# Encoder block, first stage: row scales from squares of the transposed x, and a new layout for x and the keys' weights

## Chip, core and metric

The kernel runs on one core of a Trainium2 chip. The metric is the device time of one execution in microseconds (us). The engines are TensorE (PE, whose weight loads the profile lists as PEld), VectorE (DVE), ScalarE (ACT), GpSimd (POOL) and SyncE (SP). Only SP issues transfers here, all on one queue that 16 DMA engines serve.

## What is computed

One encoder block over 512 tokens of width 1024 with 16 learned "meta" tokens ahead of them, in f32. The first stage is an RMS norm and a wide projection whose column blocks feed two attention branches; gates, a merge and a feed-forward part follow.

```python
def rms_norm(x, g):
    xf = x.astype(jnp.float32)
    y = xf * lax.rsqrt(jnp.mean(xf * xf, axis=-1, keepdims=True) + RMS_EPS)
    return (y * g.astype(jnp.float32)).astype(x.dtype)
...
    u = rms_norm(h, pre_mix_gain[l])
    proj = u @ w_in[l]
    qa, ka, va, qb, kb, vb, g = jnp.split(proj, SPLITS, axis=-1)
...
    o_swa = windowed_gqa_sink_attention(qa, ka, va, attn_sink[l], pos, is_real)
...
    o_diff = differential_attention(qb, kb, vb, lam, lambda_init, subln_gain, is_key)
    gates = jax.nn.sigmoid(g + b_gate[l])
    merged = g_swa * (o_swa @ w_branch_swa[l]) + g_diff * (o_diff @ w_branch_diff[l])
    h = h + rms_norm(merged @ w_out[l], post_mix_gain[l])
    u = rms_norm(h, pre_ffn_gain[l])
    gate_up = u @ w_ffn_in[l]
    f = (jax.nn.silu(gate_up[..., :D_FF]) * gate_up[..., D_FF:]) @ w_ffn_out[l]
    h = h + rms_norm(f, post_ffn_gain[l])
```

The row scale, one number per token, is the reciprocal root of the mean square of that token's 1024 values. It commutes with the projection, so the kernel multiplies the projected columns by it afterwards.

## The kernel before

**Products.** Every f32 operand is split into a high part of type F32R and a low part, the remainder; a product is three matmuls, high by high, high by low and low by high (`mm3`, lines 287 to 289). ACT makes the high part (`act.copy`, or `act.activation` with the gain), DVE or POOL the low part (`sub_hi`, line 253). The tokens stand transposed in `xh` and `xl` (128 partitions of features, 8 tiles of k, 528 columns: 16 meta tokens and 512 tokens).

**The front** is the part up to line 505, whose order is written out by hand for PE, ACT, DVE and SP. SP fetches the transposed x tile by tile (`x_load`, line 391, raw tiles `xr`, 264 KB each), and in between the weights of two column blocks of the keys (`w_part`, line 406). ACT and DVE split each x tile (`x_split`, lines 397 and 398) and each piece of the weights (line 257 on ACT, 253 on DVE). PE first runs 60 matmuls on a constant tile (line 380), then the keys' products k by k: 12 matmuls of 264 columns for each of 8 k (line 447), into three banks `pr` and one `Sw`. Then come the first value block with the weights `wV` (two halves `pV`, 48 matmuls) and the second with `wV2` (`pV2`, 48 matmuls).

**The row scales before.** SP fetches the 512 tokens a second time, not transposed (`xn`, line 419, four transfers of 512 KB), and the meta tokens (`xm`, line 420). ACT (line 460) and DVE (line 462) square them in turn and sum along each row into `ss`. `rsqrt_cols` (lines 306 to 318, DVE with one POOL power) turns the sums into scales; DVE spreads each over 128 columns (`rb`, lines 483 and 486) and PE transposes these into `rps` (lines 484 and 487), from where ACT copies them to `rbc`, the scale of each column.

**Behind the front** a planner takes over: `Plan` places tasks by modelled costs, by priorities and by the time at which each engine is taken to be free, a small table of numbers at the call. Its first tasks scale the value blocks by `rbc` (`VT`, line 589), transpose them on PE (lines 599 and 607), turn the keys by the rotary tables (`rope_t`, line 554 to 566), move them between partitions (`move`, line 576), fetch and split the query weights (`weights`, lines 527 and 529), and run the queries' products (512 columns a matmul). The first scores are the matmuls `Sw<-KK,Q` of line 715.

Of the kernel before, what the change touches and what calls it, by code (L numbers as in the profile page):

```python
# [237 lines left out]
def encoder(ctx, tc, I, out, dbg=None):  # L238
# [151 lines left out]
    def x_load(k):  # L390
        sp.dma_start(out=xr[k // 2][:, k % 2], in_=I["xT"][k])
        if k == 0:
            sp.dma_start(out=vec, in_=I["vec"])

    def x_split(k):
        r = xr[k // 2][:, k % 2]
        act.activation(out=xh[:, k, :], in_=r, func=AF.Copy, scale=mgain[:, k:k + 1])
        dve.scalar_tensor_tensor(out=xl[:, k, :], in0=r, scalar=mgain[:, k:k + 1],
                                 in1=xh[:, k, :].bitcast(F32), op0=ALU.mult, op1=ALU.subtract)

    def w_part(w, n, k0, k1):
        if k0 == 0:
            w.extend([wp.tile([P, KT, P], F32, tag="wr", name="wr", bufs=RB),
                      wp.tile([P, KT, P], F32R, tag="wh", name="wh"), wp.tile([P, KT, P], F32R, tag="wl", name="wl")])
        ks = slice(k0, k1)
        sp.dma_start(out=w[0][:, ks], in_=I["w_in"][n].rearrange("p (k c) -> p k c", k=KT)[:, ks])
        split(w[1][:, ks], w[2][:, ks], w[0][:, ks])

    wA, wB = [], []
    for k in range(KT):  # L410
        x_load(k)
        x_split(k)
        for k0, k1 in {0: ((0, 2),), 1: ((2, 4),), 3: ((4, KT),)}.get(k, ()):
            w_part(wA, 0, k0, k1)
            w_part(wB, 1, k0, k1)
    wA, wB = wA[1:], wB[1:]
# [22 lines left out]
    kB = [pr_t(HALF), Sw[0][:, 0:HALF]]  # L439
    halves = [slice(s * HALF, (s + 1) * HALF) for s in range(2)]  # L440
    for k in range(KT):
        todo = [(ps_, w[a][:, k, :], (xh, xl)[b][:, k, cs], k == 0 and a == b == 0, k == KT - 1 and a == 1)
                for hs, w in ((kA, wA), (kB, wB)) for ps_, cs in zip(hs, halves) for a, b in ((0, 0), (0, 1), (1, 0))]
        if k == 0:
            todo = [x for p in range(3) for x in todo[p::3]]
        for ps_, a, b, first, last in todo:
            pe.matmul(out=ps_, lhsT=a, rhs=b, start=first, stop=last)
# [8 lines left out]
    for t in range(5):
        src, n = (xn[:, t], P) if t < 4 else (xm, NMETA)
        jk = atp.tile([P, D], BF16, tag="rt", name="jk", bufs=RT)
        if t % 2 == 0:
            act.activation(out=jk[:n], in_=src, func=AF.Square, accum_out=ss[:n, t:t + 1])  # L460
        else:
            dve.tensor_tensor_reduce(out=jk[:n], in0=src, in1=src, scale=1.0, scalar=0.0,
                                     op0=ALU.mult, op1=ALU.add, accum_out=ss[:n, t:t + 1])
        if t == 0:
            for ps_, raw in ((kA, kraw[0]), (kB, kraw[1])):
                for s in range(2):
                    act.copy(out=raw[:, halves[s]], in_=ps_[s])
    pV2 = [pr_t(HALF), pr_t(HALF)]

    def v2(h, ks):  # L470
        for k in ks:
            mm3(pV2[h], (wV2[0][:, k, :], wV2[1][:, k, :]), (xh[:, k, halves[h]], xl[:, k, halves[h]]), k == 0, k == KT - 1)

    ks = [slice(h * KT // 2, (h + 1) * KT // 2) for h in range(2)]
    for h in range(2):
        act.copy(out=wV2[0][:, ks[h]], in_=rV2[:, ks[h]])
    rst = rsqrt_cols(const, ss, P, 1.0 / D, "r0",
                     between=lambda: sub_hi(wV2[1][:, ks[0]], rV2[:, ks[0]], wV2[0][:, ks[0]]))
    v2(0, range(KT // 2))
    rps = ps.tile([P, 512], F32, tag="av", name="rps")  # L480
    for t in range(4):
        rb = atp.tile([P, P], F32, tag="rt", name="rb", bufs=RT)
        dve.tensor_copy(out=rb, in_=rst[:, t:t + 1].broadcast_to([P, P]))
        pe.transpose(out=rps[:, t * P:(t + 1) * P], in_=rb, identity=ident)
    rb = atp.tile([P, P], F32, tag="rt", name="rb", bufs=RT)
    dve.tensor_copy(out=rb, in_=rst[:, 4:5].broadcast_to([P, P]))
    pe.transpose(out=Sw[1][:, 0:P], in_=rb, identity=ident)
    sub_hi(wV2[1][:, ks[1]], rV2[:, ks[1]], wV2[0][:, ks[1]])
    v2(0, range(KT // 2, KT))
    v2(1, range(KT))  # L490
# [1119 lines left out]
```

## Time and profile before

| what | value |
|---|---|
| time, median of 3 runs | 949.36 us (948.16 to 950.43) |
| time of the profiled execution | 949.22 us |
| its span, first to last instruction | 947.4 us |
| PE busy / DVE busy / ACT busy / POOL busy | 931.6 / 716.2 / 525.8 / 216.0 us |
| mean granted TensorE clock | 0.996 |
| fetched and moved by DMA | 110.46 MB, mean 117 GB/s |

Times in the rows of the trace count from the span's start. A row of the timeline gives start, duration, engine, line, operation, output and inputs, shapes, and in brackets the idle time ahead of it with what ended that idle time. Matmuls overlap, so the distance of two starts is what one costs. A duration of DVE or ACT is likewise longer than the distance to the next start.

### The profile page before, as it was taken

The numbers are of one execution on the slowest core, as the hardware profiler recorded it, in microseconds if no ns is written. First come the engines' busy times: TensorE is split into PE (matmuls) and PEld (weight loads), VectorE is DVE, ScalarE is ACT, GpSimd is POOL, SyncE is SP. The second block draws the span as 40 slices with busy tenths as digits, with TensorE's granted clock in tenths as the row PEclk, the third lists the DMA queues.
The fourth block names the chain that finished last, engine by engine and source line by source line (L and its number), as shares of the span: only waits on it lengthen the run. The fifth ranks groups of instructions, "written<-read, shape, count | busy, mean of one in ns | idle before, by whom it ended". The sixth has DMA issues, their size and how long they took to land.

```text
span 947.4 us, 15653 instructions
## 1 busy us (share of the span) xinstructions
PE 931.6 (98%) x5871; PEld 834.1 (88%) x5871; DVE 716.2 (76%) x1234; ACT 525.8 (55%) x957; POOL 216.0 (23%) x228
## 2 busy tenths in 40 slices
PE   9999999999999999999999999999999999999996
PEld 9788879889898999999888888998999999988885
DVE  5738898999564759877773865886787887799975
ACT  7337766775644446667556443654555555565541
POOL 0544455543222433243211421300000000000000
PEclk9999999999999999999999999999999999999999
DMA  9483132251425144433532460364323333180122
GB/s 319 160 220 102 51 104 58 63 148 45 123 89 157 46 122 127 105 96 115 157 112 67 161 216 23 100 186 141 117 104 101 117 95 112 46 333 13 55 67 89
DMA packets 38011, 110.46 MB, mean 117 GB/s; under 512 B 6177, under 2 KB 7457, under 8 KB 37937
## 3 DMA queue, kind: packets, MB, share of 16 engines
q1 hardware_dynamic: 37792, 109.34, 38.1%
q8 instruction: 46, 0.75, 0.3%
q14 instruction: 29, 0.23, 0.1%
q10 hardware_dynamic: 144, 0.13, 0.0%
HBM read 88.09 MB, written 2.10 MB: 95 GB/s over the span
## 4 chain that ended last, share of the span: by engine, by line
PE 86%; DVE 5%; DMA 4%; ACT 2%; issue 1%; SPq 1%; DVEq 0%; ACTq 0%
PE pr L287 19%; PE pr L289 19%; PE pr L288 19%; PE Sd L863 3%; PE wk L288 2%; PE wk L287 2%; PE wk L289 2%; PE Sw L715 2%; PE O L771 2%; PE tr L918 2%; PE Od L931 2%; PE tr L764 2%; DMA wr<-in_w_in_dram 2%; PE tr L288 1%; PE tr L287 1%; PE tr L289 1%
## 5 line engine op out<-in xcount | busy, mean ns | idle before, releaser
L287 PE MATMUL pr<-xh,wh 128*128 128x264 f32 (+1 forms) x592 | 193.4, 327 | 0.0
L289 PE MATMUL pr<-xh,wl 128*128 128x264 f32 (+1 forms) x592 | 190.0, 321 | 0.6 <-POOL wl L253 0.6
L288 PE MATMUL pr<-xl,wh 128*128 128x264 f32 (+1 forms) x592 | 189.8, 321 | 0.0
L253 POOL TENSOR_TENSOR wl<-wr,wh 128x1024 fp32r<-128x1024 f32 (+2 forms) x42 | 99.5, 2372 | 145.2 <-ACT wh L529 82.5
L289 PEld LDWEIGHTS pr<-xh,wl 128*128 128x128 f32 x592 | 111.6, 189 | 9.6 <-POOL wl L253 1.3
L288 PEld LDWEIGHTS pr<-xl,wh 128*128 128x128 f32 x592 | 111.9, 189 | 7.4
L287 PEld LDWEIGHTS pr<-xh,wh 128*128 128x128 f32 x592 | 111.8, 189 | 7.4 <-issue 0.2
L529 ACT CAST wh<-wr 128x1024 fp32r<-128x1024 f32 x56 | 58.5, 1048 | 47.0 <-PE pr L288 34.6
L309 POOL TENSOR_TENSOR r3y<-r3v,mhalf 128x1 f32<-128x1 f32 x4 | 2.2, 549 | 326.1 <-DVE r3v L308 326.1
L253 DVE TENSOR_TENSOR wl<-wr,wh 128x1024 fp32r<-128x1024 f32 (+2 forms) x61 | 69.0, 1134 | 10.0 <-ACT wh L272 8.2
L287 PE MATMUL pr<-TM,sx 128*128 128x256 f32 x236 | 66.9, 283 | 0.2 <-ACT s L1393 0.2
L289 PE MATMUL pr<-TM,sx 128*128 128x256 f32 x236 | 66.8, 283 | 0.0
L288 PE MATMUL pr<-TM,sx 128*128 128x256 f32 x236 | 66.8, 283 | 0.0
L868 DVE TENSOR_REDUCE nm<-Sd 128x1 f32<-128x528 f32 x64 | 45.1, 705 | 20.8 <-PE Sd L863 19.9
L253 DVE TENSOR_TENSOR sx<-S,sx 128x1024 fp32r<-128x1024 f32 x34 | 41.6, 1224 | 24.9 <-PE pr L288 12.7
L289 PE MATMUL pr<-uh,wl 128*128 128x256 f32 (+1 forms) x188 | 55.0, 292 | 0.4 <-DVE wl L253 0.4
L287 PE MATMUL pr<-uh,wh 128*128 128x256 f32 (+1 forms) x188 | 55.0, 293 | 0.0
L288 PE MATMUL pr<-ul,wh 128*128 128x256 f32 (+1 forms) x188 | 54.9, 292 | 0.0
L566 POOL TENSOR_TENSOR ta<-ta,tb 128x528 f32<-128x528 f32 (+1 forms) x26 | 37.0, 1422 | 74.5 <-DVE tb L554 45.3
L871 ACT ACTIVATE pp<-Sd,nm 128x528 f32<-128x528 f32 x40 | 27.9, 699 | 39.2 <-DVE pa L884 22.6
L257 ACT CAST sx<-S 128x1024 fp32r<-128x1024 f32 x34 | 35.7, 1050 | 25.1 <-PE pr L289 8.2
L729 POOL TENSOR_SCALAR p<-p,rc 128x272 f32<-128x272 f32 (+1 forms) x64 | 35.9, 573 | 47.9 <-DVE rc L727 44.5
(528 smaller groups left out, 2673.9 us busy)
## 6 DMA issues: line engine op xcount, KB each, us to landing
wr<-in_w_in_dram SPq DMA_DIRECT2D x50, 512.0 KB, 4.1
wg<-in_w_fi_dram SPq DMA_DIRECT2D x17, 512.0 KB, 3.6
wu<-in_w_fi_dram SPq DMA_DIRECT2D x17, 512.0 KB, 3.5
wr<-in_w_fi_dram SPq DMA_DIRECT2D x16, 512.0 KB, 3.8
b<-in_w_fo_dram SPq DMA_DIRECT2D x16, 512.0 KB, 8.5
Kd<-hl SPq DMA_DIRECT2D x32, 132.0 KB, 2.4
Kd<-Kd SPq DMA_DIRECT2D x16, 264.0 KB, 3.7
Q<-hl SPq DMA_DIRECT2D x64, 64.0 KB, 2.8
```

The costliest lines, as they stand in the source:

```text
L253: (eng or dve).tensor_tensor(out=lo, in0=src, in1=hi.bitcast(F32), op=ALU.subtract)
L257: act.copy(out=hi, in_=src)
L287: pe.matmul(out=ps, lhsT=ah, rhs=bh, start=first, stop=False, **more)
L288: pe.matmul(out=ps, lhsT=ah, rhs=bl, start=False, stop=False, **more)
L289: pe.matmul(out=ps, lhsT=al, rhs=bh, start=False, stop=last, **more)
L529: T("ACT", 1.05, lambda: act.copy(out=wh.t, in_=wr.t), r=[wr], w=[wh], prio=pr_)
L566: T("POOL", 0.05 + 1.3 * m, lambda: pool.tensor_tensor(out=ta.t[:, :, 0:n], in0=ta.t[:, :, 0:n], in1=tb.t[:, :, 0:n], op=ALU.add), r=[tb], ...
L715: pe.matmul(out=Sw2[S.slot][:, 0:nk], lhsT=QS[g][hh].t[:, i * P:(i + 1) * P], rhs=KB[g].t[:, x, r0:r1], start=(x == 0), stop=(x == 1))
L729: T("POOL", 0.2 + 0.43 * c, lambda z=z: pool.tensor_scalar(out=pt.t[:, z, 0:nk], in0=pt.t[:, z, 0:nk], scalar1=rc.t[:, z:z + 1], scalar2=1 ...
L863: pe.matmul(out=S.t[:, s, 0:HALF], lhsT=Q[c].t[:, i * P:(i + 1) * P], rhs=K[c].t[:, x, s * HALF:(s + 1) * HALF], start=(x == 0), stop=(x = ...
L868: T("DVE", 0.71, lambda S=S, c=c, one=one: dve.tensor_reduce(out=nm.t[:, c, one], in_=S.t[:, :, 0:HALF], axis=AX.XY, op=ALU.min), r=[S], w ...
L871: T("ACT", 0.9, lambda S=S, c=c, one=one, p=p: act.activation(out=p().rearrange("p (a b) -> p a b", a=2), in_=S.t[:, :, 0:HALF], func=AF.E ...
```

## The change

1. The second fetch of the tokens and the fetch of the meta tokens are gone (five transfers, 2,112 KB), and with them the row sums on ACT and DVE.
2. The squares now come from the raw transposed tiles `xr`: four ACT squares of 128x1056, which DVE adds up to one tile of 128x1056 in three additions. PE sums over the partitions: ten matmuls with a piece of that tile as the stationary operand and one column of ones as the moving one, in plain f32, written to a PSUM bank that is again called `ss`.
3. `xT` is stored with the partitions outermost, so that tiles 2 and 3, 4 and 5, 6 and 7 come in one transfer each (528 KB, 4,224 B a partition). The weights of the two key blocks are stored side by side (`w_k`) and come in five transfers of 128, 128, 256, 256 and 256 KB, in place of six.
4. The first value block runs half by half (`v1`), the second half behind the transposes of the scales. The second value block is no longer part of the front: the planner places its products, and its weights are split in one piece.
5. The planner's table says PE 1.2 and DVE 2.0, in place of 4.3 and 0.05.

```diff
-    xn = big.tile([P, 4, D], F32, tag="t1", name="xn")
-    xm = big.tile([NMETA, D], F32, tag="oh", name="xm")
+    sq = big.tile([P, 3, 2, EXT], F32, tag="t1", name="sq")
+    sq = [sq[:, i] for i in range(3)] + [big.tile([P, 2, EXT], F32, tag="oh", name="sq3")]
...
+    def x_load(k0, k1):
+        sp.dma_start(out=xr[k0 // 2][:, k0 % 2:k0 % 2 + k1 - k0], in_=I["xT"][:, k0:k1])
...
+    def square(i):
+        act.activation(out=sq[i], in_=xr[i], func=AF.Square)
+
+    def add(i, j):
+        dve.tensor_tensor(out=sq[i], in0=sq[i], in1=sq[j], op=ALU.add)
+
+    for k0, k1 in ((0, 1), (1, 2), (2, 4), (4, 6), (6, 8)):
+        x_load(k0, k1)
         if k0 == 0:
...
+            sp.dma_start(out=vec, in_=I["vec"])
+        for k in range(k0, k1):
+            x_split(k)
+        k_weights(k0, k1)
+        if k0 == 4:
+            square(0)
+        if k0 == 6:
+            square(1)
+    add(0, 1)
     wV = load_w(I["w_in"][2], dst=[atp.tile([P, KT, P], F32R, tag="p", name="wV", bufs=2) for _ in range(2)])
-    for t in range(4):
-        sp.dma_start(out=xn[:, t], in_=I["x"][t * P:(t + 1) * P])
-    sp.dma_start(out=xm, in_=I["meta"])
+    square(2)
+    square(3)
+    add(2, 3)
+    add(0, 2)
...
+    ss = ps.tile([P, 512], F32, tag="av", name="ss")[:, 0:5]
+    for t in range(5):
+        c0 = NMETA + t * P if t < 4 else 0
+        for x in range(2):
+            pe.matmul(out=ss[:, t:t + 1], lhsT=sq[0][:, x, c0:c0 + P], rhs=ones[:, 0:1].bitcast(F32), start=(x == 0), stop=(x == 1))
...
+    v1(0)
...
+    rst = rsqrt_cols(const, ss, P, 1.0 / D, "r0")
...
+    v1(1)
+    act.copy(out=wV2[0], in_=rV2)
...
-                   ta=2, tb=1, vt=1, rt=RT, ma=3), dict(PE=4.3, ACT=0.05, DVE=0.05, POOL=0.0, SP=0.0))
+                   ta=2, tb=1, vt=1, rt=RT, ma=3), dict(PE=1.2, ACT=0.05, DVE=2.0, POOL=0.0, SP=0.0))
...
-    v_swa(PV2)
+    v_swa([products(w3, X, X_, h * HALF, (h + 1) * HALF) for h in range(2)])
```

What this does to the order of ACT, from the split of x tiles 4 and 5 on; in the change:

```order
L396 ACTIVATE xh<-xr,vec 128x528 x2
L257 CAST wh<-wr 128x512
L408 ACTIVATE sq<-xr 128x1056
L396 ACTIVATE xh<-xr,vec 128x528 x2
L257 CAST wh<-wr 128x512
L408 ACTIVATE sq<-xr 128x1056
L272 CAST wV<-wr 128x1024
L408 ACTIVATE sq<-xr 128x1056
L408 ACTIVATE sq_159<-xr 128x1056
L476 COPY kraw<-pr 128x264 x3
```

The four squares stand between and behind the splits of x and of the weights; the last of them is behind the cast of `wV`. Before, the row sums of line 460 stood behind that cast.

On DVE, from the same place on, in the change:

```order
L397 SCALAR_TENSOR_TENSOR xl<-xr,vec,xh 128x528 x2
L253 TENSOR_TENSOR wl<-wr,wh 128x512
L397 SCALAR_TENSOR_TENSOR xl<-xr,vec,xh 128x528 x2
L253 TENSOR_TENSOR wl<-wr,wh 128x512
L411 TENSOR_TENSOR sq<-sq 128x1056
L253 TENSOR_TENSOR wV<-wr,wV 128x1024
L411 TENSOR_TENSOR sq<-sq,sq_159 128x1056
L411 TENSOR_TENSOR sq<-sq 128x1056
L306 TENSOR_SCALAR r0v<-ss 128x5
```

Two of the three additions stand behind the last square, and the second of these needs the first.

On PE, at the end of the keys' products (line 458 is line 447 of before), in the change:

```order
L458 MATMUL Sw<-xh,wl 128x264
L463 MATMUL ss<-ones,sq 128x1 x10
L469 MATMUL tr<-xh,wV 128x264 x8
L469 MATMUL tr<-xl,wV 128x264 x8
L469 MATMUL tr<-xh,wV 128x264 x8
L482 MATMUL rps<-ident,rb 128x128 x4
L482 MATMUL Sw<-ident,rb 128x128
L469 MATMUL tr<-xh,wV 128x264 x8
```

The ten new matmuls stand straight behind the keys, ahead of all value products; before, the value products followed there, and PE had no part in the sums. The transposes of the scales now stand in the middle of the first value block; before they stood in the second. Further on, by the planner, the four transposes of the second scaled value block (line 607) stand behind fifteen query matmuls of 512 columns, where there were six. Behind the 153 query matmuls that precede the first scores, the order of PE is the same in both kernels.

More of the change, by code (lines that the diff above doesn't have):

```diff
@@ L385, in encoder @@
     X = (xh, xl)
-    xn = big.tile([P, 4, D], F32, tag="t1", name="xn")
-    xm = big.tile([NMETA, D], F32, tag="oh", name="xm")
+    sq = big.tile([P, 3, 2, EXT], F32, tag="t1", name="sq")
+    sq = [sq[:, i] for i in range(3)] + [big.tile([P, 2, EXT], F32, tag="oh", name="sq3")]
     xr = [zp.tile([P, 2, EXT], F32, tag="kk", name="xr", bufs=4) for _ in range(4)]
[L390 to L393, printed above, removed]
+    wK = []
+    def x_load(k0, k1):
+        sp.dma_start(out=xr[k0 // 2][:, k0 % 2:k0 % 2 + k1 - k0], in_=I["xT"][:, k0:k1])
     def x_split(k):
@@ L399, in x_split @@
                                  in1=xh[:, k, :].bitcast(F32), op0=ALU.mult, op1=ALU.subtract)
-    def w_part(w, n, k0, k1):
-        if k0 == 0:
[L403 to L416, printed above, removed]
-    wV = load_w(I["w_in"][2], dst=[atp.tile([P, KT, P], F32R, tag="p", name="wV", bufs=2) for _ in range(2)])
-    for t in range(4):
-        sp.dma_start(out=xn[:, t], in_=I["x"][t * P:(t + 1) * P])
-    sp.dma_start(out=xm, in_=I["meta"])
+    def k_weights(k0, k1):
+        if k0 % 4 == 0:
+            wK.append([wp.tile([P, 4, 2, P], dt, tag=t, name=t, bufs=RB) for t, dt in (("wr", F32), ("wh", F32R), ("wl", F32R))])
+        w = [t[:, k0 % 4:k0 % 4 + k1 - k0] for t in wK[-1]]
+        sp.dma_start(out=w[0], in_=I["w_k"].rearrange("p (k a c) -> p k a c", k=KT, a=2)[:, k0:k1])
+        split(w[1], w[2], w[0])
@@ L421, in encoder @@
+    add(0, 1)
+    wV = load_w(I["w_in"][2], dst=[atp.tile([P, KT, P], F32R, tag="p", name="wV", bufs=2) for _ in range(2)])
+    square(2)
+    square(3)
+    add(2, 3)
+    add(0, 2)
+    sp.dma_start(out=ident, in_=I["ident"])
     nw[0] += 1
     rV2 = wp.tile([P, KT, P], F32, tag="wr", name="wr", bufs=RB)
-    wV2 = [wp.tile([P, KT, P], F32R, tag=t, name=t) for t in ("wh", "wl")]
+    wV2 = [wp.tile([P, KT, P], F32R, tag=t, name=t, bufs=RB) for t in ("wh", "wl")]
     sp.dma_start(out=rV2, in_=I["w_in"][3].rearrange("p (k c) -> p k c", k=KT))
-    sp.dma_start(out=ident, in_=I["ident"])
@@ L441, in encoder @@
     for k in range(KT):
-        todo = [(ps_, w[a][:, k, :], (xh, xl)[b][:, k, cs], k == 0 and a == b == 0, k == KT - 1 and a == 1)
-                for hs, w in ((kA, wA), (kB, wB)) for ps_, cs in zip(hs, halves) for a, b in ((0, 0), (0, 1), (1, 0))]
+        _, wh, wl = wK[k // 4]
+        w = (wh[:, k % 4], wl[:, k % 4])
+        todo = [(ps_, w[a][:, n, :], (xh, xl)[b][:, k, cs], k == 0 and a == b == 0, k == KT - 1 and a == 1)
+                for n, hs in enumerate((kA, kB)) for ps_, cs in zip(hs, halves) for a, b in ((0, 0), (0, 1), (1, 0))]
         if k == 0:
@@ L447, in encoder @@
             pe.matmul(out=ps_, lhsT=a, rhs=b, start=first, stop=last)
-    pV = [tr_t()[:, 0:HALF], tr_t()[:, 0:HALF]]
-    for h in range(2):
-        proj(pV[h], wV, X, h * HALF, (h + 1) * HALF)
-    kraw = [atp.tile([P, EXT], F32, tag="q", name="kraw", bufs=8) for _ in range(2)]
-    ss = const.tile([P, 5], F32, name="ss")
-    pool.memset(ss, 1.0)
-    for t in range(5):
[L457 to L478, printed above, removed]
@@ L479, in encoder, with v1 @@
-    v2(0, range(KT // 2))
-    rps = ps.tile([P, 512], F32, tag="av", name="rps")
-    for t in range(4):
+    ss = ps.tile([P, 512], F32, tag="av", name="ss")[:, 0:5]
[3 more added lines that the diff above has]
+            pe.matmul(out=ss[:, t:t + 1], lhsT=sq[0][:, x, c0:c0 + P], rhs=ones[:, 0:1].bitcast(F32), start=(x == 0), stop=(x == 1))
+    pV = [tr_t()[:, 0:HALF], tr_t()[:, 0:HALF]]
+    def v1(h):
+        for a, b in ((0, 0), (0, 1), (1, 0)):
+            for k in range(KT):
+                pe.matmul(out=pV[h], lhsT=wV[a][:, k, :], rhs=X[b][:, k, halves[h]], start=(a == b == k == 0),
+                          stop=(a == 1 and k == KT - 1))
@@ L482, in encoder @@
+    v1(0)
+    kraw = [atp.tile([P, EXT], F32, tag="q", name="kraw", bufs=8) for _ in range(2)]
+    for ps_, raw in ((kA, kraw[0]), (kB, kraw[1])):
+        for s in range(2):
+            act.copy(out=raw[:, halves[s]], in_=ps_[s])
+    rst = rsqrt_cols(const, ss, P, 1.0 / D, "r0")
+    rps = ps.tile([P, 512], F32, tag="av", name="rps")
+    for t in range(5):
         rb = atp.tile([P, P], F32, tag="rt", name="rb", bufs=RT)
         dve.tensor_copy(out=rb, in_=rst[:, t:t + 1].broadcast_to([P, P]))
-        pe.transpose(out=rps[:, t * P:(t + 1) * P], in_=rb, identity=ident)
@@ L485, in encoder @@
[L485 to L490, printed above, removed]
+        pe.transpose(out=rps[:, t * P:(t + 1) * P] if t < 4 else Sw[1][:, 0:P], in_=rb, identity=ident)
+    v1(1)
+    act.copy(out=wV2[0], in_=rV2)
     act.copy(out=rbc[:, NMETA:EXT], in_=rps)
@@ L492, in encoder @@
     act.copy(out=rbc[:, 0:NMETA], in_=Sw[1][:, 0:NMETA])
+    sub_hi(wV2[1], rV2, wV2[0])
     pool.tensor_scalar(out=hb, in0=vec[:, 8:24], scalar1=0.5, scalar2=1.0, op0=ALU.mult, op1=ALU.mult)
@@ L579, in encoder @@
     X_ = []
-    for t in ("wh", "wl"):
-        pl.slots[t][0] = 4.4
+    w3 = [pl.held(t, x) for t, x in zip(("wh", "wl"), wV2)]
     def v_scaled(pv):
@@ L647, in encoder @@
     PV = [pl.held("tr", t) for t in pV]
-    PV2 = [pl.held("pr", t) for t in pV2]
     for b in MK:
@@ L1555, in prepare @@
     d = {}
-    d["xT"] = f(np.concatenate([meta, x], 0).T).reshape(KT, P, EXT)
-    d["x"], d["meta"] = f(x), f(meta)
+    d["xT"] = f(np.concatenate([meta, x], 0).T.reshape(KT, P, EXT).transpose(1, 0, 2))
+    d["x"] = f(x)
     d["w_in"] = _tiles(a["w_in"][0], _in_cols())
+    d["w_k"] = f(d["w_in"][:2].reshape(2, P, KT, P).transpose(1, 2, 0, 3)).reshape(P, 2 * D)
     allc = np.arange(D)
```

## The prediction

> **What bounds the kernel now.** First the page's busy times and its chain of waits: PE is busy nearly throughout, and most of the chain that ended last is matmuls. A change of the front counts only as far as it moves PE.
>
> ```profile
> PE 931.6 (98%) x5871; PEld 834.1 (88%) x5871; DVE 716.2 (76%) x1234; ACT 525.8 (55%) x957; POOL 216.0 (23%) x228
> PE 86%; DVE 5%; DMA 4%; ACT 2%; issue 1%; SPq 1%; DVEq 0%; ACTq 0%
> ```
>
> Then the waits of PE, and PE's timeline from the first product to the first scores. The gaps in it are all that the change can win there.
>
> ```profile
> 9.23 0.28 PE L447 MATMUL pr<-xh,wh 128*128 128x264 f32 x1
> 9.74 0.39 PE L447 MATMUL pr<-xl,wh 128*128 128x264 f32 x1 [0.23 <-DVE xl L398]
> ...
> 12.67 0.28 PE L447 MATMUL pr<-xh,wh 128*128 128x264 f32 x1
> 13.31 0.39 PE L447 MATMUL pr<-xl,wh 128*128 128x264 f32 x1 [0.37 <-DVE xl L398]
> ...
> 18.98 0.28 PE L447 MATMUL Sw<-xh,wl 128*128 128x264 f32 x1
> 19.10 0.28 PE L287 MATMUL tr<-xh,wV 128*128 128x264 f32 x1
> ...
> 32.10 0.40 PE L288 MATMUL pr<-xl,wh 128*128 128x512 f32 x1
> 32.79 0.50 PE L289 MATMUL pr<-xh,wl 128*128 128x512 f32 x1 [0.29 <-POOL wl L253]
> ...
> 33.35 0.39 PE L288 MATMUL pr<-xl,wh 128*128 128x512 f32 x1
> 33.59 0.39 PE L289 MATMUL pr<-xh,wl 128*128 128x512 f32 x1
> 35.62 0.90 PE L607 MATMUL tr<-ident,VT 128*128 128x128 f32 x4 [1.65 <-DVE Vm L628]
> ...
> 38.89 0.41 PE L599 MATMUL tr<-ident,vr 128*128 128x128 f32 x1
> 38.95 0.61 PE L287 MATMUL pr<-xh,wh 128*128 128x512 f32 x1
> ...
> 72.54 0.76 PE L715 MATMUL Sw<-KK,Q 128*128 128x272 f32 x4 [0.50 <-DMA Q<-hl]
> ```
>
> By distances of starts, a 264-column matmul costs 0.12 us (18.98 to 19.10) and a 512-column one 0.23 (about 33.35 to 33.59). So the gaps are 0.39 and 0.52 in the keys' stage, 0.46 at 32.79 and 1.80 at 35.62, where PE waits for the second scaled value block. The second fetch of the tokens stands in none of these waits by name; it delays the weights and scales that end two of them. Behind that gap the granted clock halves:
>
> ```profile
> 36.00:37.00 1.00, 1.00 (x5) 0.50 0.00 0
> 37.00:38.00 1.00, 1.00 (x3) 0.50 0.00 0
> 39.00:40.00 1.00, 1.00 (x6) 0.87 0.28 20
> ```
>
> From 35.62 to 38.95, 3.33 us, PE does four transposes, six 512-column matmuls and one transpose. At full clock these are 5 x 0.11 + 6 x 0.23 = 1.93 (0.11: the transposes below). The **clock drop** costs 1.4.
>
> **The change: when the new sums are ready.** The squares stand in line on ACT, so I follow ACT, then DVE. The rows that price them:
>
> ```profile
> 8.14 1.44 ACT L397 ACTIVATE xh<-xr,vec 128x528 fp32r<-128x528 f32 x2 [0.77 <-DMA xr<-in_xT_dram]
> 11.72 2.86 ACT L397 ACTIVATE xh<-xr,vec 128x528 fp32r<-128x528 f32 x4
> 17.16 1.06 ACT L460 ACTIVATE jk<-xn 128x1024 bf16<-128x1024 f32 x1 [0.29 <-DMA xn<-in_x_dram]
> 18.13 0.19 ACT L460 ACTIVATION_READ_ACCUMULATOR jk<-xn 128x1 f32 x1
> 23.01 1.12 ACT L476 CAST wh<-wr 128x512 fp32r<-128x512 f32 x2
> 58.68 1.22 DVE L253 TENSOR_TENSOR wl<-wr,wh 128x1024 fp32r<-128x1024 f32 x1
> 59.81 0.68 DVE L554 TENSOR_TENSOR tb<-pr,rot 128x512 f32<-128x512 f32 x1
> 6.00:9.00 3.00, 1.00 0.92 280
> 11.00:19.00 8.00, 1.00 1.03 414
> ```
>
> Landing first. Before, tile 2 of x was on chip at 8.14, when 1,325 KB had been asked for (x 3 x 264, weights 2 x 256, the vector 21). In the change tiles 2 and 3 land together, after 1,333 KB: the same place in the stream. What may help is the length of the rows: the queue moved 280 GB/s from 6 to 9 us (1 and 2 KB rows) and 414 from 11 to 19 (4 KB rows), so 528 KB in 4 KB rows take 1.3 us in place of 1.9. I take 7.5, with 7.0 and 8.1 as ends.
>
> From there ACT never waits for more than a tenth: six splits of x at 0.71 (2.86 less the last one's 0.74, over 3), three casts of 512 at 0.51 (1.12 less 0.61), the cast of `wV` at 0.97 and four squares of 1056 at 1.0 (0.97 from 17.16 to 18.13, by 1056/1024). That is 4.3 + 1.5 + 1.0 + 4.0 = 10.8, so the last square is done at 18.3. DVE then has two dependent additions of 1056 (1.13 from 58.68 to 59.81, so 1.2 and at the end 1.3 with the way out): **20.85**. Everything else of DVE's list is done before.
>
> The keys' products hardly change. Their third k now needs weights that are split behind both x tiles: low part out at about 10.4 against PE at 9.35, a stall of 1.05 in place of 0.39 + 0.52. They end at 19.25. PE then waits 1.6 for the sums. To the first of the ten new matmuls the change is 20.85 - 19.10 = **+1.75** (ends +1.2 and +2.4, from the landing).
>
> **The ten matmuls.** No row shows a plain f32 product with one moving column. The stationary operand is that of the transposes:
>
> ```profile
> 26.40 0.60 PE L484 MATMUL rps<-ident,rb 128*128 128x128 f32 x4
> 26.84 0.27 PE L487 MATMUL Sw<-ident,rb 128*128 128x128 f32 x1
> ```
>
> 0.11 each, so 1.1 for ten. The other end is what the kernel pays for a full f32 product out of three passes: 3 x 0.12 = 0.36, so 3.6. I take 0.2 each, nearer to the transposes because there is hardly anything to stream: **+2.0**. [...]
>
> **Behind it.** From the sums to the last spread scale it took 2.85 us before:
>
> ```profile
> 23.14 0.17 DVE L306 TENSOR_SCALAR r0v<-ss 128x5 f32<-128x5 f32 x1 [0.29 <-ACT jk L460]
> ...
> 25.23 0.64 DVE L483 COPY rb<-r0y 128x128 f32<-128x128 f32 x4
> 25.77 0.22 DVE L486 COPY rb<-r0y 128x128 f32<-128x128 f32 x1
> ```
>
> In the change the first half of the value block, 24 x 0.12 = 2.9 us of PE, lies over that: 0. The split of `wV2` on ACT and DVE lies under the second half, another 2.9: 0. The query weights come 2.1 MB earlier in the queue, so POOL's low part is no longer late: **-0.46**. For the second scaled value block I follow DVE, whose rows of before are these:
>
> ```profile
> 28.76 3.98 POOL L253 TENSOR_TENSOR wl<-wr,wh 128x1024 fp32r<-128x1024 f32 x1
> ...
> 28.69 1.80 DVE L653 TENSOR_TENSOR rot<-rot,rbc 128x1584 f32<-128x1584 f32 x1
> 30.53 2.77 DVE L554 TENSOR_TENSOR ta<-kraw,rot 128x528 f32<-128x528 f32 x1
> 33.22 0.70 DVE L554 TENSOR_TENSOR tb<-kraw,rot 128x528 f32<-128x528 f32 x1
> 33.84 0.69 DVE L554 TENSOR_TENSOR ta<-kraw,rot 128x528 f32<-128x528 f32 x1
> 34.46 0.76 DVE L589 TENSOR_TENSOR VT<-pr,rbc 128x264 f32<-128x264 f32 x2
> ```
>
> PE: 20.85 + 2.0, two half blocks (2.9 each), ten transposes (1.1) around `wV2`'s 48 matmuls (5.8), fifteen query matmuls (3.5): it wants the block at 39.0. DVE: after the first block's second half (29.2) come VT 0.4, rot 1.8, a wait for the transposed first block until 32.2 and its low part 0.6, three rotary products at 0.7, VT 0.4, a query weight's low part 1.1, a rotary product 0.7, VT 0.4: 37.7, or 1.3 before. So this gap goes: **-1.80**. The clock drop of before goes with its gap (**-1.4**). A gap of 1.6, with ten tiny matmuls behind it, is like the one of before, 1.80, so I charge one at the new place: **+1.4**. The keys' moves and the queries' moves come behind the same scales, shifted about as PE is: the 0.50 at 72.54 stays, within 0.5 each way.
>
> Sum: 1.75 + 2.0 - 0.46 - 1.80 - 1.4 + 1.4 = **+1.5**. The profiled execution took 949.22, span 947.4, close to the median of 949.36. So **950.7**. A difference under 0.2% (1.9 us, 947.5 to 951.3) is about what a measurement of this kernel cannot tell from no change.
>
> **Rivals.** *No clock drop* (0.27): the same walk with the clock kept, 949.3. For it: the gaps of 0.39 and 0.52 brought none, and part of the new time is matmuls, not idle. Against it: 1.80 was enough once. [...]
>
> *Faster* (0.11): sums at the early end (+1.2), matmuls at the transposes' price (1.1), no drop, and the 0.50 at the scores gone: 1.2 + 1.1 - 0.46 - 1.8 - 1.4 - 0.5 = -1.9, so 947.3. It needs all ends at once.
>
> *Slower* (0.17): the wait for the second scaled block comes back. In DVE's rows above the first rotary product runs beside POOL's subtraction for a query weight. It took 2.77 where the next took 0.70: 2.1 more. It decides from the point at which POOL is still subtracting when DVE reaches that product. Then the 1.3 of cover is gone, PE waits 0.8 and pays a second drop of 1.4: +3.7, so 952.9.
>
> *The change does not do what it says*: the second fetch was waited for through the scales, and these come no earlier now. That is the forecast itself, not another time.
>
> **How the numbers follow.** Forecast 0.45, no drop 0.27, faster 0.11, slower 0.17. The range takes the forecast with the dear matmuls (+1.6) and most of the slower case, up to 953.0, and down to 947.6, between no drop with cheap matmuls (948.4) and the faster case; some 0.07 lies below and 0.11 above. Faster by over 0.2%: half of the faster case and a little of the second, 0.08. Slower by over 0.2%: the slower case and a third of the forecast's, 0.30. The rest, 0.62, is no change.
>
> **What would show it.** In the changed profile: x tiles 2 and 3 on ACT near 7.5; the last square out near 18.3; PE idle 1 to 2.4 us at the ten matmuls, released by DVE's addition; these at 0.1 to 0.36 each; the clock at 0.5 for some 3 us behind them; no wait at the second transposes. A PE that finds the sums ready, or a front stage with new gaps behind the scales, would make the prediction wrong.

## The result and the profile after

| | before | after |
|---|---|---|
| median | 950.09 us (6 runs) | 956.98 us (6 runs, 954.62 to 959.44) |
| ratio | | 1.0068, 95% interval 1.0044 to 1.0092 |
| profiled execution, its span | 949.22, 947.4 us | 959.44, 957.6 us |
| first scores, in the profiled execution | 72.54 us | 81.27 us |

The change is slower by 0.7%, and the time lies above the predicted range. The profiled execution of the changed kernel is the slowest of its six, so its rows are set beside a second one below.

PE's timeline of the changed kernel, with the idle time ahead of a row and what ended it in brackets; the rows stand at the places of those shown of before:

```profile
10.81 0.39 PE L458 MATMUL pr<-xh,wh 128*128 128x264 f32 x1 [1.02 <-ACT wh L257]
11.57 0.39 PE L458 MATMUL pr<-xh,wl 128*128 128x264 f32 x1 [0.26 <-DVE wl L253]
...
22.73 4.15 PE L463 MATMUL ss<-ones,sq 128*128 128x1 f32 x20 [2.42 <-DVE sq L411]
26.73 2.11 PE L469 MATMUL tr<-xh,wV 128*128 128x264 f32 x8
28.64 1.68 PE L469 MATMUL tr<-xl,wV 128*128 128x264 f32 x8
30.16 1.14 PE L469 MATMUL tr<-xh,wV 128*128 128x264 f32 x8
31.14 0.60 PE L482 MATMUL rps<-ident,rb 128*128 128x128 f32 x4
...
39.23 0.33 PE L593 MATMUL tr<-ident,vr 128*128 128x128 f32 x1 [0.73 <-POOL vr L591]
...
46.96 0.55 PE L601 MATMUL tr<-ident,VT 128*128 128x128 f32 x3 [1.24 <-DVE VT L583]
...
81.27 0.74 PE L708 MATMUL Sw<-KK,Q 128*128 128x272 f32 x4 [1.64 <-DMA Q<-hl]
```

Four things are to be seen. PE is idle for 2.42 us ahead of the sums. The ten matmuls are twenty in the trace and take 4.00 us until the next row (26.73 - 22.73). The first half of the value block takes 4.41 us (31.14 - 26.73), where 24 matmuls at 0.12 are 2.9. Waits of 0.73, 1.24 and 1.64 follow.

The stretches of the same stage; the columns are the stretch and its length, the busy share of PE, PEld, DVE, ACT and POOL, the granted clock, and DMA:

```profile
22.00:23.00 1.00, 0.27 (x3) 0.30 (x3) 0.58 (x1) 0.97 (x2) 0.00 (x0) 1.00 0.50 201
23.00:24.00 1.00, 1.00 (x7) 1.00 (x6) 0.00 (x0) 0.12 (x1) 0.00 (x0) 0.50 0.02 8
...
29.00:30.00 1.00, 1.00 (x7) 1.00 (x6) 1.00 (x6) 0.00 (x0) 0.00 (x0) 0.58 0.00 0
30.00:31.00 1.00, 1.00 (x10) 1.00 (x9) 0.89 (x1) 0.00 (x0) 0.00 (x0) 1.00 0.00 0
```

The clock is halved from 23.0 to 29.84 (a mean of 0.58 over 29 to 30 is 0.84 us at one half), that is for 6.84 us, twice the 3.4 of the drop in the kernel before. It covers nearly all of the sums and most of the half value block.

What released the sums, on ACT and DVE:

```profile
8.70 1.36 ACT L396 ACTIVATE xh<-xr,vec 128x528 fp32r<-128x528 f32 x2 [1.64 <-DMA xr<-in_xT_dram]
11.49 1.36 ACT L396 ACTIVATE xh<-xr,vec 128x528 fp32r<-128x528 f32 x2 [0.73 <-DMA xr<-in_xT_dram]
...
17.94 2.05 ACT L408 ACTIVATE sq<-xr 128x1056 f32<-128x1056 f32 x2
...
20.03 1.26 DVE L411 TENSOR_TENSOR sq<-sq,sq 128x1056 f32<-128x1056 f32 x1 [0.50 <-ACT sq L408]
21.32 1.26 DVE L411 TENSOR_TENSOR sq<-sq 128x1056 f32<-128x1056 f32 x1
```

Tiles 2 and 3 reach ACT at 8.70, and ACT waits again for tiles 4 and 5. The last square is out at 20.0 and the sum tile at 22.6.

POOL and DVE around the second waits:

```profile
34.98 2.38 POOL L253 TENSOR_TENSOR wl<-wr,wh 128x1024 fp32r<-128x1024 f32 x1
37.30 1.87 POOL L591 COPY vr<-VT 128x128 f32<-128x128 f32 x1
...
43.17 2.83 POOL L253 TENSOR_TENSOR wl<-wr,wh 128x1024 fp32r<-128x1024 f32 x1 [0.50 <-ACT wh L524]
...
35.16 3.87 DVE L646 TENSOR_TENSOR rot<-rot,rbc 128x1584 f32<-128x1584 f32 x1
...
43.67 2.89 DVE L549 TENSOR_TENSOR tb<-kraw,rot 128x528 f32<-128x528 f32 x1
46.49 0.42 DVE L583 TENSOR_TENSOR VT<-pr,rbc 128x264 f32<-128x264 f32 x1
```

DVE's product took 1.80 in the kernel before and 3.87 here; it starts 0.18 behind POOL's subtraction and ends at 39.03, which is 1.67 behind the subtraction's end (37.36). POOL's copy, 0.29 in the kernel before (line 597, at 28.50), starts at 37.30 and ends at 39.17, 0.14 behind the product. The same happens at 43: DVE's `tb` ends 0.56 behind POOL (46.56 against 46.00) and the scaled block `VT`, for which PE waits, stands behind it. In these rows the later of the two ends about as far behind the other's end as it took in the kernel before: 1.67 against 1.80, 0.14 against 0.29, 0.56 against 0.70. Why the two hang together is not shown.

### The profile page after: what moved, and what is told of

Read it like the earlier page. It is cut to its first block, busy times and chain, and to the rows that moved or that the text cites. A ratio compares the mean times of both kernels' runs of the same rounds, so it can differ in the third digit from the quotient of the medians.

```text
span 957.6 us, 15662 instructions
## 1 busy us (share of the span) xinstructions
PE 936.8 (98%) x5891; PEld 838.8 (88%) x5891; DVE 719.4 (75%) x1231; ACT 525.4 (55%) x953; POOL 216.0 (23%) x227
## 4 chain that ended last, share of the span: by engine, by line
PE 85%; DVE 6%; DMA 3%; ACT 2%; SPq 2%; issue 1%; DVEq 0%; ACTq 0%
PE pr L287 19%; PE pr L289 19%; PE pr L288 19%; PE Sd L856 3%; PE wk L288 2%; PE wk L287 2%; PE wk L289 2%; PE Sw L708 2%; PE O L764 2%; PE tr L757 2%; PE tr L911 2%; SPq L571 1%; PE Od L924 1%; PE tr L289 1%; PE tr L287 1%; PE tr L288 1%
```

## The experiments

All ratios are to the kernel before, whose runs are shared by the kernels of one session: 951.18 us (22 runs) for the first four, 950.94 (23) for the next four, 950.46 (23) for the three after that, and 950.63 (17) for the last.

| label | what it is | median us | ratio, 95% interval | first scores in its profile |
|---|---|---|---|---|
| e0_again | the changed kernel again | 957.27 | 1.0060, 1.0043 to 1.0077 | 80.10 |
| e1_later | ten sums behind the half value block | 952.96 | 1.0016, 1.0003 to 1.0029 | 75.85 |
| e2_oldorder | older order of transfers | 957.48 | 1.0065, 1.0044 to 1.0085 | 79.69 |
| e3_five | five sums | 955.28 | 1.0038, 1.0024 to 1.0052 | 78.38 |
| e4_fill | PE kept busy ahead of the sums | 958.30 | 1.0075, 1.0048 to 1.0101 | 77.61 |
| e5_port | e1_later, two low parts on DVE | 962.41 | 1.0114, 1.0091 to 1.0137 | 74.86 |
| e6_five_old | e1_later, five sums, older order | 949.55 | 0.9985, 0.9972 to 0.9999 | 72.56 |
| e7_table | e1_later, planner's table as measured | 953.81 | 1.0032, 1.0015 to 1.0048 | 76.34 |
| e8_bdm | e6_five_old, `bdm` cleared on ACT | 949.75 | 0.9988, 0.9978 to 0.9998 | 72.69 |
| e9_layout | the kernel before with the new layout | 951.61 | 1.0007, 0.9996 to 1.0019 | 73.69 |
| e10_fill_five | e4_fill with five sums | 954.83 | 1.0046, 1.0028 to 1.0065 | 76.04 |
| e11_later_five | e1_later with five sums | 949.92 | 0.9997, 0.9985 to 1.0008 | 75.59 |

### The changed kernel again (e0_again)

> The changed kernel once more, for a second profile and a narrower time. If the gap at the ten sums is the cause (theory 1), PE again idles 2 to 3 us ahead of them, released by DVE's last addition, and the clock is at 0.5 for 3.4 or 6.8 us behind it; 955 to 959 us. If the long profile was an accident of that execution (rival), the gap or the half clock is missing and the time is near 951.

957.27 us: the result is repeated. PE's timeline:

```profile
22.36 3.30 PE L463 MATMUL ss<-ones,sq 128*128 128x1 f32 x20 [2.48 <-DVE sq L411]
25.52 2.11 PE L469 MATMUL tr<-xh,wV 128*128 128x264 f32 x8
```

And the stretch in which the clock changes:

```profile
23.00:24.00 1.00, 1.00 (x9) 1.00 (x9) 0.00 (x0) 0.58 (x1) 0.00 (x0) 0.78 0.00 0
```

The wait is the same, but the clock halves later, at 23.56 (a mean of 0.78), when the sums are already running, and these take 3.16. Tiles 2 and 3 of x reach ACT at 7.83 here, 0.9 earlier than in the first profile, and tiles 4 and 5 0.4 earlier:

```profile
11.11 1.36 ACT L396 ACTIVATE xh<-xr,vec 128x528 fp32r<-128x528 f32 x2 [0.76 <-DMA xr<-in_xT_dram]
```

The sums start 0.37 earlier. They follow the second pair of tiles and not the first.

### The sums moved behind PE's value products (e1_later)

```diff
-    ss = ps.tile([P, 512], F32, tag="av", name="ss")[:, 0:5]
-    for t in range(5):
...
     v1(0)
...
+    ss = ps.tile([P, 512], F32, tag="av", name="ss")[:, 0:5]
+    for t in range(5):
...
+        if t == 0:
+            v1(1)
```

> The ten sums stand behind the first half of the first value block, and the second half runs ahead of the transposes of the scales. Theory 1 (the place on PE): the 24 value matmuls cover the wait of 2.6 us, no half clock at the sums, so these cost 2.0 in place of 4.0 and the value products 1.5 less: about 6 us faster than the changed kernel, near 951. Theory 2 (late landing of x) alone: the gap shrinks by what is covered, but the end of the keys' products stays at 20.1 and only some 2.6 us are won, near 954.5. Theory 3 (the sums themselves are dear): they still take 4 us and 953 to 954 is left.

```profile
23.77 2.29 PE L472 MATMUL ss<-ones,sq 128*128 128x1 f32 x20
25.92 1.23 PE L464 MATMUL tr<-xh,wV 128*128 128x264 f32 x8
...
35.57 0.33 PE L594 MATMUL tr<-ident,vr 128*128 128x128 f32 x1 [1.69 <-POOL vr L592]
...
75.85 0.82 PE L709 MATMUL Sw<-KK,Q 128*128 128x272 f32 x4 [1.35 <-DMA Q<-hl]
```

No wait stands at the sums, the twenty passes take 2.15, and the clock is 1.00 from 20 to 24 and from 26 to 31 us. The median falls by 4.3 us (957.27 to 952.96), the first scores come 4.25 earlier. Most of the loss, 4.3 of 6.1 us (957.27 less 951.18), is the place on PE. The 951 of theory 1 is missed by 2: waits of 1.69 for `vr`, 1.35 for `Q` and, at 252 us, 1.03 for `Qd` are left.

### The order of transfers (e2_oldorder)

x comes tile by tile in the new layout, and the key weights come in three transfers, in the order of the kernel before.

```diff
-    for k0, k1 in ((0, 1), (1, 2), (2, 4), (4, 6), (6, 8)):
-        x_load(k0, k1)
+    for k in range(KT):
+        x_load(k, k + 1)
```

> x tile by tile and the keys' weights in pieces of 2, 2 and 4 k, in the order of before, from the new layout; the squares and sums as in the changed kernel. Theory 2 (the transfers in pairs land later): tile 2 is on ACT near 8.1 in place of 8.7, the keys end about 0.7 earlier, the sums 0.6 to 1.2 earlier: 1 to 2 us faster than the changed kernel. Theory 1: the gap at the sums stays at 2 us or more and the half clock with it; less than 1 us won.

```profile
21.83 3.73 PE L463 MATMUL ss<-ones,sq 128*128 128x1 f32 x20 [2.16 <-DVE sq L411]
```

The sums start 0.5 to 0.9 earlier than in the two profiles of the changed kernel, the first scores come 0.4 to 1.6 earlier, and the median is the same. The late landing does not carry the loss.

### Half as many passes (e3_five)

```diff
+    dve.tensor_tensor(out=sq[0][:, 0], in0=sq[0][:, 0], in1=sq[0][:, 1], op=ALU.add)
...
-        for x in range(2):
-            pe.matmul(out=ss[:, t:t + 1], lhsT=sq[0][:, x, c0:c0 + P], rhs=ones[:, 0:1].bitcast(F32), start=(x == 0), stop=(x == 1))
+        pe.matmul(out=ss[:, t:t + 1], lhsT=sq[0][:, 0, c0:c0 + P], rhs=ones[:, 0:1].bitcast(F32), start=True, stop=True)
```

> DVE folds the two halves of the added squares once more (128x528, 0.7 us), so PE does five sums in place of ten. Theory 3 (two passes for each plain f32 product): ten loads in place of twenty, 2.0 us less at half clock, 0.7 more wait: about 1.3 us faster than the changed kernel. Theory 1: the wait grows by 0.7 and the half clock stays; between 1.5 faster and no difference. If a sum is one pass and half of the 4.15 us is waiting, no gain and 0.7 slower.

```profile
23.16 2.27 PE L463 MATMUL ss<-ones,sq 128*128 128x1 f32 x10 [2.88 <-DVE sq L430]
25.29 2.11 PE L469 MATMUL tr<-xh,wV 128*128 128x264 f32 x8
```

Five products are ten passes, 2.13 us at half clock. The wait grows to 2.88, and the time falls by 2.0 all the same, more than the 1.3 of theory 3. A plain f32 product with one moving column thus stands in the trace as two matmuls, called passes here: 0.11 each at full clock (2.15 for twenty, e1_later) and 0.21 at half.

### PE kept busy in the wait (e4_fill, e10_fill_five)

```diff
+    for _ in range(45):
+        pe.matmul(out=wps[:, 0:P], lhsT=warm, rhs=warm, start=True, stop=True)
     ss = ps.tile([P, 512], F32, tag="av", name="ss")[:, 0:5]
```

> The changed kernel with 45 more matmuls on the constant tile (128x128, as at the kernel's start, result unused) between the keys' products and the ten sum matmuls, so that TensorE has work while it waits for the squares. Theory A (the half clock is a cost of its own): the 45 matmuls are full-length work of about 0.06 to 0.1 us each at full clock and lie inside the idle 2.5 us or a little beyond it; the granted clock stays 1.0 through the ten sums and the first value block; the ten sums' twenty passes take 2.0 us in place of 3.3 to 4.0, the value block wins 1.5; time 953.5, 3 to 4 below the changed kernel. Rival B (the time is lost to the wait and to the passes themselves, and the half clock lies over waits of other engines that come later anyway): the time stays within 1 us of the changed kernel, 956 to 958. Rival C (the many matmuls run past the squares): the first scores come later than in the changed kernel.

> The changed kernel with five sums (the edit of e3_five) and the 45 matmuls on the constant tile of e4_fill. Theory A (half clock costs time wherever it falls): no half clock from 20 to 30 us, five sums at 1.0 us in place of 2.0, the value block at full clock, first scores at 76, 2.5 earlier than in e3_five; time 952.5 to 953.3 against 955.3. Rival B (what the kept clock wins is lost at later waits, as in e4_fill, where the first scores came 2.5 to 3.7 earlier and 5.0 was lost at one wait for Qd at 474 with a clock drop behind it): first scores near 76 but time 955 or more, and the profile shows where.

PE's timeline of e4_fill:

```profile
20.45 2.69 PE L460 MATMUL wps<-warm 128*128 128x128 bf16 x45
...
23.24 2.36 PE L465 MATMUL ss<-ones,sq 128*128 128x1 f32 x20
...
77.61 0.74 PE L710 MATMUL Sw<-KK,Q 128*128 128x272 f32 x4 [0.68 <-DMA Q<-hl]
...
474.42 0.77 PE L858 MATMUL Sd<-Kd,Qd 128*128 128x264 f32 x4 [3.26 <-DMA Qd<-hl]
```

The stretches from 20 to 28 us, with the granted clock in the third column from the right:

```profile
20.00:24.00 4.00, 3.90 (x58) 3.70 (x57) 2.52 (x2) 3.28 (x7) 0.00 (x0) 1.00 0.53 162
24.00:28.00 4.00, 4.00 (x36) 4.00 (x36) 1.11 (x7) 1.04 (x1) 1.20 (x1) 1.00 0.02 4
```

The clock stays at 1.00, and the first scores come 2.5 (against e0_again) to 3.7 earlier, as theory A said; with five sums 2.3 earlier (76.04 against 78.38). But the medians are 958.30 and 954.83, no better than 957.27 and 955.28: rival B. In e4_fill PE later waits 3.26 for `Qd` and the clock halves behind that (0.50 from 475 to 476 us); in e10_fill_five the waits are 0.86 at 252 and 0.72 at 470, both for `Qd`, and 1.00 at 667. The unfilled kernels have no such wait at 470. So the half clock costs some 2.5 us at the first scores, and a kernel that only keeps the clock and leaves the sums where they are does not keep the gain. Why those transfers land later there stays open. The wait at 474 can't be the whole of it: the profiled execution, 960.70, is 2.4 above the median, and the three shortest, at 957.3, are still as long as the unfilled kernel.

### VectorE against GpSimd (e5_port, e8_bdm)

e5_port gives two subtractions of POOL's to DVE, in e1_later. e8_bdm gives POOL's clearing of `bdm` to ACT, in e6_five_old.

```diff
-        if nfill[0] % 2:
+        if nfill[0] % 2 and nfill[0] > 3:
```

```diff
-        pool.tensor_copy(out=bd1[:, c * 256:(c + 1) * 256], in_=zero)
+        act.copy(out=bd1[:, c * 256:(c + 1) * 256], in_=zero)
```

> The kernel with the ten sums behind the first half of the value block (e1_later), with the low parts of the first and the third query weights on VectorE in place of GpSimd. Theory A (VectorE and GpSimd hold each other up at the spread scales): VectorE's long rotary product takes 1.8 us in place of 3.2, GpSimd's copy vr 0.3 in place of 0.8, the wait of 1.69 for vr shrinks below 0.7, and the time falls by 1.0 to 1.7 below e1_later, to about 951.5. Rival B (GpSimd's work is needed where it is, VectorE becomes late): a wait for wl or VT on TensorE of 1 us or more takes its place, time as e1_later or longer, 953 to 955.

> e6_five_old with the two casts that clear bdm on ScalarE, behind the copies of the scales, in place of GpSimd. Nothing else moves in the order. In e6_five_old they took 2.32 us on GpSimd (30.67 to 32.94) while VectorE ran its long rotary product (3.20 us, 1.80 in the kernel before), and TensorE then waited 1.68 us for the copy vr behind them. Theory A (GpSimd and VectorE hold each other up): the product falls to 1.8 to 2.4 us, vr is ready before 32.1, the wait of 1.68 falls below 0.3, and the time falls by 1.3 to 1.7, to 947.9 to 948.3, 0.997 of the kernel before. Rival B (vr is late for another reason, or the next wait takes its place): another wait of 1 us or more by 43 us, time 949 to 950.

e5_port is 9.5 us over e1_later, far worse than either theory. At the place itself the wait for `vr` fell from 1.69 to 0.73 and a wait of 0.42 for VT came, but the planner orders the rest differently from there: its profile has waits of 1.61 (369 us), 1.29 (449) and 1.62 (453), and a mean granted clock of 0.993 against 0.999 in the one of e1_later. It tells nothing on the long rows of DVE and POOL. The order of e8_bdm differs from that of e6_five_old by the two casts alone. Its rows of POOL and DVE, and then of PE:

```profile
28.02 2.39 POOL L253 TENSOR_TENSOR wl<-wr,wh 128x1024 fp32r<-128x1024 f32 x1
30.34 1.87 POOL L592 COPY vr<-VT 128x128 f32<-128x128 f32 x1
...
28.86 3.20 DVE L647 TENSOR_TENSOR rot<-rot,rbc 128x1584 f32<-128x1584 f32 x1
...
32.27 0.33 PE L594 MATMUL tr<-ident,vr 128*128 128x128 f32 x1 [0.46 <-POOL vr L592]
...
40.00 0.55 PE L602 MATMUL tr<-ident,VT 128*128 128x128 f32 x3 [1.24 <-DVE VT L584]
```

The wait for `vr` falls from 1.68 to 0.46, and 1.24 for VT takes its place (the product `tb` stood 2.89 beside the next subtraction). That is rival B: 949.75 against 949.55. The product still takes 3.20 with the subtraction beside it (it ends 1.65 behind that) and no `bdm`: the theory had the wrong pair. Here the wait that became shorter brought the next one in its place.

### The planner's table (e7_table)

```diff
-                   ta=2, tb=1, vt=1, rt=RT, ma=3), dict(PE=1.2, ACT=0.05, DVE=2.0, POOL=0.0, SP=0.0))
+                   ta=2, tb=1, vt=1, rt=RT, ma=3), dict(PE=0.0, ACT=0.05, DVE=0.05, POOL=0.0, SP=0.0))
```

> e1_later with the planner's table at the times that its trace shows (TensorE 0.0, VectorE 0.05 in place of 1.2 and 2.0). The key moves then stand in the queue four ahead of and four behind a query weight, as in the kernel before; in the changed kernel all eight stand behind four weights. Theory A (the waits for Q and Qd at the scores, 1.35 and 1.03 in e1_later, are due to the order in which the table puts the moves): both waits fall below 0.6, time 1 to 1.7 below e1_later, 951.3 to 952. Rival B (the moves' producers are late, and their place in the queue does not matter): the waits stay over 1.0, time as e1_later, 952.5 to 953.5.

The waits stay, 1.20 for `Q` and 1.27 for `Qd`, and the time is 953.81: rival B, with the time 0.3 over its range. The place of the keys' moves in the queue is not what makes them late.

### Layout alone, and the sums put right (e9_layout, e6_five_old, e11_later_five)

e9_layout is the kernel before with point 3 of the change only. e11_later_five is e1_later with the edit of e3_five; e6_five_old adds the edit of e2_oldorder.

> The kernel before with the new layout alone: x tiles 2 and 3, 4 and 5, 6 and 7 paired, key weights side by side in five transfers; the second fetch of the tokens, the row sums and all orders behind stay as they were. Theory A (the paired landing makes the third k's weights late, and otherwise the layout is worth nothing): the keys' waits sum to 1.3 to 1.8 us in place of 0.9 to 1.0, the time is 0.3 to 0.8 over the kernel before, ratio 1.0003 to 1.001, not to be told from it. Rival B (fewer, longer transfers bring everything behind them earlier): the wait of 1.65 at the second transposes shrinks, time 1 to 2 under the kernel before. Rival C (the longer wait halves the clock in the keys' stage, as in two of the profiles): 1.4 to 2 over it.

> e1_later with VectorE folding the two halves of the squares (five sums of ten passes in place of ten of twenty) and with the older order of transfers (x tile by tile in the new layout, weights in three transfers). If twenty passes at full clock cost 0.1 each: five sums win 1.0. If the waits in the keys' stage are those of the paired transfers: another 0.5 to 0.8. Sum: 951.2 to 951.6. If the passes overlap with the products at full clock, or the wait at vr only grows by what is won: as e1_later, 952.5 to 953.3.

> e1_later with five sums of ten passes, the transfers paired as in the changed kernel: what of the 3.4 us between e1_later (952.96) and e6_five_old (949.55) is the five sums, and what the older order of transfers. Theory A (the fold is worth its passes, 1.0, and takes the waits for Q and Qd with it, as in e3_five; the older order wins the 0.7 of the keys' waits): the waits for Q and Qd fall below 0.5, time 950.3 to 951. Theory B (the older order of transfers is what removes the waits for Q and Qd): these waits stay over 0.8, time 951.5 to 952.3. Rival C (the paired transfers' longer waits in the keys' stage halve the clock in some executions): a half clock of 3.4 us between 12 and 16 us, and 1.5 more.

e9_layout, PE's timeline:

```profile
36.26 0.63 PE L607 MATMUL tr<-ident,VT 128*128 128x128 f32 x4 [1.64 <-DVE Vm L628]
...
73.69 0.86 PE L715 MATMUL Sw<-KK,Q 128*128 128x272 f32 x4 [2.59 <-DMA Q<-hl]
```

951.61 against 950.46, an interval that holds 1: the layout alone is worth nothing that can be told, as theory A said. The 1.64 at the second transposes is the old one, and here the clock did not halve behind it. The first scores come no earlier for that: PE waits 2.59 for `Q` where it waited 0.50 in the kernel before.

e11_later_five takes 949.92, 3.0 under e1_later, or 1.8 by the ratios to the kernel before, as the two stand in different sessions: 1.1 of it is the ten passes saved (2.15 less 1.03), and the waits for `Q` and `Qd`, 1.35 and 1.03, are gone. The older order on top (e6_five_old, 949.55, where 951.2 to 951.6 was expected) gives nothing to speak of, so theory A holds for the fold and not for the order. The profiled execution of e11_later_five, 952.16 and among its slowest, also shows rival C, with a half clock of twice the length. PE's timeline:

```profile
11.22 0.59 PE L459 MATMUL pr<-xh,wh 128*128 128x264 f32 x1 [2.03 <-ACT wh L257]
```

And the stretches around it:

```profile
10.00:11.00 1.00, 0.00 (x0) 0.00 (x0) 1.00 (x2) 0.97 (x2) 0.00 (x0) 0.92 1.06 416
11.00:12.00 1.00, 0.78 (x2) 0.50 (x2) 0.98 (x2) 0.23 (x2) 0.00 (x0) 0.50 1.01 405
...
17.00:18.00 1.00, 1.00 (x8) 1.00 (x7) 0.93 (x2) 1.00 (x2) 0.00 (x0) 0.67 0.45 188
```

A wait of 2.03 for the paired tiles and their weights, and half clock from 10.84 to 17.66. Of its twelve executions, the three with a mean clock of 0.996 or less took 950.79 to 952.40 us, the eight with 0.998 or more 948.89 to 950.50. With the older order (e6_five_old) no execution is under 0.997.

## Why the prediction was wrong

The step that failed is the price of the sums at the place where the change puts them. The prediction charged 1.75 us for their later start, 2.0 for the ten matmuls and 1.4 for a half clock behind them, 5.15 together; the profile has 3.63, 4.00 and 1.5, 9.13 together. The runs show in its place that PE waits for the sums, that the half clock lies over the sums themselves, and that the same sums behind half of the value block (e1_later) give back 4.3 of the 6.1 us lost. The waits for `vr`, VT, `Q` and `Qd`, put at nothing, come on top.

The path to the first scores carries 8.73 us (81.27 - 72.54) of the 10.22 between the two profiled executions; behind it stands the wait of 1.47 for `Qd` at 258. The medians lie 6.9 apart, for the profiled execution of the changed kernel is 2.5 above its median. The predicted terms against the rows:

| term | predicted | in the changed kernel's profile |
|---|---|---|
| start of the sums, against 19.10 | +1.75 (1.2 to 2.4) | +3.63 (e0_again +3.26) |
| ten matmuls | +2.0 (1.1 to 3.6) | +4.00 (e0_again +3.16) |
| half clock over the products behind | +1.4 | +1.5 (4.41 less 2.9) |
| POOL's low part, second transposes, old drop | -0.46, -1.80, -1.4 | -0.46, -1.80, -1.4 |
| new waits for `vr`, and for VT, at the second transposes again | none | +0.73, +1.24 |
| wait at the scores | 0, within 0.5 | +1.14 (1.64 less 0.50) |
| sum | +1.5 | +8.58 of 8.73 |

The +0.73 and +1.24 are idle times of the rows. By distances of starts, as the prediction counts its gaps, they are 0.89 and 1.40, and the sum is 8.90.

**The start of the sums.** What failed here is "ACT never waits for more than a tenth". ACT waited 0.73 for tiles 4 and 5 and had them at 11.49, where the prediction's own walk needs them by 9.4 (7.5, two splits and a cast). ACT does not wait again behind this landing, and the sums follow it: in the nine profiles with paired transfers and squares the last addition starts 9.83 or 9.84 us behind it (11.49 and 21.32 in the changed kernel, 11.11 and 20.95 in e0_again, 11.87 and 21.70 in e1_later). So the last square came at 20.0, not 18.3, and PE waited 2.42, not 1.6. "I take 7.5, with 7.0 and 8.1 as ends" was off as well (7.83 and 8.70, in e1_later 9.40), but PE did not wait for it. The rate of 414 GB/s, from a stretch of whole 8 us, did not give the landing of the pairs: a 528 KB transfer of x landed 7.5 us after its issue and a 264 KB one, before, after 5.1 (medians of the DMA issues on the two pages). e2_oldorder shows that the landing alone was worth little in the end.

**The ten matmuls and the clock.** These were two terms and are one. At full clock the size was right: 2.15 in e1_later against 2.0. It is the drop that was mis-sized. It was charged as one of 3.4 us behind the sums; it lasted 6.84 and lay over the sums themselves, which took 4.00. The trace has two matmuls for each product, most of them at half clock here. That a drop would come was right: the rival that keeps the clock did not occur in any of the four profiles with the sums at this place and no fill.

**Not costed together: place and wait.** e1_later shows what the step "PE then waits 1.6" overlooked. At the place where the change put the sums, every us of their delay became PE's. Half of the value block, ready on PE's side, covers the whole wait.

**The second transposes.** The old gap and the drop behind it went, as predicted. But the cover of 1.3 at VT (1.5 by the prediction's own terms, which add up to 37.5 and not 37.7) did not hold, and the "slower" rival named the rows: a DVE product beside POOL's subtraction (`tb`, 2.89 here against 0.70 in the kernel before). Such a pair was found once more, at `rot` and `vr`, where no rival had put it. Its second drop did not come.

**The scores.** That "the 0.50 at 72.54 stays" failed: 1.64, and a further 1.47 for `Qd` at 258. Neither shows in the profiles of three kernels with five sums (e3_five, e6_five_old, e11_later_five); in a fourth, e10_fill_five, 0.22 and 0.86 are left, and in e7_table both stay. In the kernel before the first scores start 4.1 us behind the issue of the last four moves of `Q` ahead of them (72.54 less 68.45), in the changed kernel 4.9 (81.27 less 76.41). The moves thus come close ahead of the scores in both, and time saved on PE alone can be lost there, as in e9_layout, where PE waits 2.59 for `Q`. What decides the waits was not settled.

**What is left of the change.** With the sums behind the half value block and folded to five, the change is at 0.9997 (0.9985 to 1.0008) of the kernel before: by the rows, the waits that it removes are paid by the passes, the keys' waits and the long rows of DVE and POOL. With the older order of transfers, and with `bdm` on ACT, it is at 0.9985 and 0.9988, with intervals just under 1. They are the fastest here, 0.8% under the changed kernel and 0.1 to 0.2% under the one before, which is hardly more than can be told.

## What to carry to other kernels

Price a new small product at the place where PE reaches it: if its input comes late, put it behind work that is ready: here a wait of 2.42 us was followed by half clock over the product itself, which took 4.00 us where it took 2.15 behind ready work. Charge the drop by its length (3.4 or 6.8 us here) over whatever lies there, not as a lump behind the gap. A better time at one mark (here the first scores) is not yet a better kernel: look at the waits that follow before counting it.

## What was not expected of the hardware

Ahead of the kernel's end, the half clock came in pieces of 3.4 us (the kernel before, e4_fill) or 6.8 (the changed kernel, e0_again, e3_five, e11_later_five), and the length of an idle time alone did not tell whether and when. It began 1.65 us into an idle time of 2.03 (e11_later_five), 0.3 behind the end of the 2.42 of the changed kernel, and 1.2 behind the end of the 2.48 of e0_again; idle times of 1.64 (e9_layout) and 1.68 (e6_five_old) brought none, by the distances of the matmuls behind them (0.23 for 512 columns, 0.12 for 264), where 1.65 did in the kernel before.

Finer stretches of the traces of the two kernels show an order in this. In the kernel before the clock halves at 35.84, is back at 39.25, and halves as the kernel ends, at 943.78; in the changed kernel it halves at 23.00, is back at 29.83, and halves at 954.84. From the first to the last of these it is 266 and 273 times 3.413 us, and the pieces of half clock are one and two of it, so that all these changes lie a whole number of 3.413 us apart, each execution with its own grid of such times. From grid line to grid line, in these two profiles, a stretch at full clock was followed by half clock where PE was busy 1.47 us of it or less (1.47 and 1.00, and 0.00 at both kernels' ends), and never where PE was busy 1.94 or more; none lay between. In the kernel before, the idle times of 1.65 and 0.29 fell into one stretch and left 1.47 busy.

Why a piece has one or two of these lengths is less clear. In the changed kernel, e0_again and e3_five it was two, and the first of the two held most or all of the sums, though PE was busy throughout it in the first two of these; a stretch at half clock with PE busy throughout was followed by full clock (35.84 in the kernel before). e11_later_five has two lengths with matmuls of 264 columns and 0.38 of idle time. What decides it, no run shows.
